# Identity shuffles in place of VectorE copies in a sliding-window kernel

## The chip, the core and the metric

One core of a Trainium2 chip. The metric is device time in microseconds (us) of one execution, the median of the runs. All runs compared here are at a granted clock of 1.00.

## The reference

All 8 x 8 windows at stride 4 of 16 x 64 images of 64 x 64 float32, copied into an output with the windows outermost:

```
n_h = (h - window_size) // stride + 1          # 15
n_w = (w - window_size) // stride + 1          # 15
for i in range(n_h):
    for j in range(n_w):
        result[:, i, j] = x[:, :, i*4 : i*4+8, j*4 : j*4+8].copy()     # 64 channels x 8 x 8
```

There is no arithmetic: 16.8 MB come in, 59 MB of windows go out.

## The kernel before

The image lies in `L`, spread over 128 partitions: 2 channel halves x 16 images x 4 bands of 16 rows. For each store tile `G` (one of four buffers, 16 KB per partition) ScalarE (`act`) and VectorE (`dve`) gather one window per partition, then GpSimd issues an indirect store that sends each partition's 16 KB to its place in the output. A unit with `s = 0` ("plain") handles windows that lie within one band in both halves. A "cross" unit (`s = 2`) pairs windows of one half within a band with windows of the other half (`s = 3`) whose last 4 rows lie in the next band, that is in the next partition; those rows are fetched by a `stream_shuffle` with the mask `nxt`. The 16 rows of a cross unit that have no window are dropped by the store's bounds check.

```
def fill(g, half, s, j, lo, n, copies):
    d = slice(half * HP + lo, half * HP + lo + n)          # 64 partitions
    cols = slice(j * ST, j * ST + WS)
    for ch in (half, 1 - half):
        ...
        copy = copies[ch != half]
        if s < NSLOT - 1:
            copy(out=g[d, cs, :, :], in_=L[f, :, s * ST : s * ST + WS, cols])       # 2048 elements
        else:
            copy(out=g[d, cs, 0:ST, :], in_=L[f, :, s * ST : RB, cols])             # 1024 elements
            nc.vector.stream_shuffle(out=g[d, cs, ST:WS, :], in_=L[f, :, 0:ST, cols], mask=nxt)

def unit(j, s):
    g = tile_()                                  # next of the 4 buffers
    if s == 0:
        for half in range(CH):
            fill(g, half, half, j, 0, HP, (act, dve))
        scatter(g, idx, j, s)
    else:
        turn = crossed % 2
        crossed += 1
        fill(g, turn, s, j, 0, HP, (act, act))
        fill(g, 1 - turn, s + 1, j, 0, HP, (dve, dve))
        scatter(g, (idx_hi, idx_lo)[turn], j, s)
# ... six early tiles, three plain units between them, then 3 cross + 1 plain, five times ...
j = NW - 1                                       # the tail: two half-filled tiles
tile_()                                          # one buffer is skipped
for s in range(2):
    g = tile_()
    # ... act and dve copy 32 x 2048 twice each; 4 stores of 256 KB from the SP and ACT queues ...
```

## Time and profile before

| | before |
|---|---|
| median of the first 3 runs (range) | 191.89 us (191.82 to 192.07) |
| VectorE busy | 120.5 us of 190.1 |
| ScalarE busy | 130.0 us |
| data moved | 75.81 MB, mean 399 GB/s |
| steady rate, 78 to 166 us | 421 GB/s |

No engine is busy even 70% of the span, while the transfer engines are busy in nearly all of it. The lines stand in the prediction.

### The profile page before, as it was taken

The page shows a single profiled execution, that of the slowest core. Times are in us where ns is not written, and L with a number is a line of the kernel's source. Part 1 is how long each engine was busy: PE and PEld are TensorE (multiplying, and loading weights), DVE is VectorE, ACT ScalarE, POOL GpSimd, SP SyncE. Part 2 cuts the span into 40 slices and gives each one's busy share as a digit, 9 for nine tenths or more (in the row PEclk, how much of TensorE's full clock was granted, in tenths as well). Part 3 has the DMA queues.
Part 4 walks back from the last instruction along what each step waited for, and adds up shares of the span by engine and source line. Part 5 has one row for each costly group of instructions (what it writes and reads, how often), then busy time and mean ns, then how long its engine had stood idle before and what let it go on. Part 6 is the DMA issues. An engine that isn't in the chain of part 4 may idle for free.

```text
span 190.1 us, 481 instructions
## 1 busy us (share of the span) xinstructions
DVE 120.5 (63%) x160; ACT 130.0 (68%) x69; POOL 49.9 (26%) x50
## 2 busy tenths in 40 slices
DVE  4000007999998969877659586795877679552420
ACT  0000007999999989977779589797877979572750
POOL 7402203205535321522322222223122431210000
DMA  2999999999999999999999999999999999999974
GB/s 83 310 408 403 398 400 396 400 401 392 438 431 431 422 424 441 417 410 417 441 397 431 426 422 414 424 438 393 438 414 417 428 424 424 405 434 410 421 331 197
DMA packets 11156, 75.81 MB, mean 399 GB/s; under 512 B 3456, under 2 KB 3456, under 8 KB 7552
## 3 DMA queue, kind: packets, MB, share of 16 engines
q0 software_dynamic: 9040, 66.34, 84.7%
q1 hardware_dynamic: 2048, 8.91, 12.0%
q10 hardware_dynamic: 64, 0.52, 0.7%
q14 instruction: 4, 0.03, 0.0%
HBM read 16.78 MB, written 62.91 MB: 419 GB/s over the span
## 4 chain that ended last, share of the span: by engine, by line
DMA 84%; DVE 6%; ACT 3%; POOL 2%; issue 1%; ACTq 0%; DVEq 0%; PEldq 0%
DMA out_dram<-G,idx_hi 30%; DMA L<-in_x_dram 20%; DMA out_dram<-G,idx 14%; DMA out_dram<-G,idx_y 13%; DMA out_dram<-G,idx_lo 7%; DVE G L166 4%; POOL L L58 2%; ACT G L212 2%; ACT G L143 1%; DVE G L146 1%; DVE G L145 0%; DVE G L143 0%; POOL pi L69 0%; ACTq L143 0%; DVEq L145 0%
## 5 line engine op out<-in xcount | busy, mean ns | idle before, releaser
L143 ACT COPY G<-L 64x2048 f32<-64x2048 f32 x46 | 87.2, 1896 | 17.0 <-DMA out_dram<-G,idx_hi 7.6
L166 DVE COPY G<-L 32x2048 f32<-32x2048 f32 x30 | 36.9, 1230 | 28.9 <-DMA L<-in_x_dram 25.9
L146 DVE STREAM_SHUFFLE G<-L 64x1024 f32<-64x1024 f32 x30 | 38.3, 1276 | 0.0
L166 ACT COPY G<-L 32x2048 f32<-32x2048 f32 x18 | 33.9, 1896 | 1.2 <-DMA out_dram<-G,idx_y 0.8
L145 DVE COPY G<-L 64x1024 f32<-64x1024 f32 x30 | 20.6, 688 | 16.4 <-DMA out_dram<-G,idx_hi 10.5
L143 DVE COPY G<-L 64x2048 f32<-64x2048 f32 x16 | 19.6, 1223 | 6.7 <-DMA out_dram<-G,idx 6.3
L166 ACT ACT_TABLE_LOAD x1 | 1.3, 1283 | 29.5 <-DMA L<-in_x_dram 29.5
L123 POOL DMA_INDIRECT out_dram<-G,idx_y x6 | 10.8, 1808 | 25.2 <-DVE G L166 24.1
L58 POOL DMA_DIRECT2D L<-in_x_dram x16 | 10.9, 695 | 24.1 <-DMA L<-in_x_dram 23.6
L123 POOL DMA_INDIRECT out_dram<-G,idx_hi x8 | 9.7, 1207 | 24.2 <-DVE G L146 12.3
L123 POOL DMA_INDIRECT out_dram<-G,idx_lo x7 | 8.0, 1144 | 29.4 <-DVE G L146 19.6
L123 POOL DMA_INDIRECT out_dram<-G,idx x8 | 10.2, 1270 | 18.0 <-ACT G L143 18.0
L212 ACT COPY G<-L 32x2048 f32<-32x2048 f32 x4 | 7.6, 1897 | 5.5 <-DMA out_dram<-G,idx_lo 4.5
L212 DVE COPY G<-L 32x2048 f32<-32x2048 f32 x4 | 4.9, 1220 | 8.2 <-DMA out_dram<-G,idx_lo 5.8
L72 DVE TENSOR_SCALAR tb<-pi 128x1 int32<-128x1 int32 x1 | 0.2, 155 | 1.0 <-POOL pi L69 1.0
L78 DVE TENSOR_TENSOR th<-tc,tq 128x1 int32<-128x1 int32 x2 | 0.3, 156 | 0.0
L75 DVE TENSOR_SCALAR th<-tc 128x1 int32<-128x1 int32 x2 | 0.3, 154 | 0.0
L69 POOL IOTA pi<- 128x1 int32 x1 | 0.1, 124 | 0.4 <-PEq L246 0.4
L146 DVE LOAD_MASK_SELECT G<-L x30 | 0.2, 6 | 0.0
L78 DVE CUSTOM_DVE_ANT_0 tb<-tb,th 128x2 uint16<-128x2 uint16 x1 | 0.2, 160 | 0.0
L78 DVE CUSTOM_DVE_ANT_0 idx_y<-idx_y,idx 128x2 uint16<-128x2 uint16 x1 | 0.2, 160 | 0.0
L78 DVE CUSTOM_DVE_ANT_0 idx<-tb,th 128x2 uint16<-128x2 uint16 x1 | 0.2, 159 | 0.0
(16 smaller groups left out, 2.2 us busy)
## 6 DMA issues: line engine op xcount, KB each, us to landing
L<-in_x_dram POOLq DMA_DIRECT2D x8, 1024.0 KB, 21.1
L<-in_x_dram SPq DMA_DIRECT2D x8, 896.0 KB
out_dram<-G SPq DMA_DIRECT2D x6, 256.0 KB
L<-in_x_dram POOLq DMA_DIRECT2D x8, 128.0 KB, 21.2
out_dram<-G ACTq DMA_DIRECT2D x2, 256.0 KB
out_dram<-G,idx POOLq DMA_INDIRECT x8, 14.7
out_dram<-G,idx_hi POOLq DMA_INDIRECT x8, 14.6
out_dram<-G,idx_lo POOLq DMA_INDIRECT x7, 12.9
```

Of the source, the lines that this page charges most:

```text
L58: eng.dma_start(out=L[p0 : p0 + QP - HQ + 1 : HQ, c0:c1, :, :], in_=x_v[ch, y, q, :, c0:c1, :])
L69: nc.gpsimd.iota(pi[:, :], pattern=[[0, 1]], base=0, channel_multiplier=1)
L72: nc.vector.tensor_scalar(out=d[:, :], in0=pi[:, :], scalar1=shift, scalar2=mask, op0=ALU.logical_shift_right, op1=ALU.bitwise_and)
L75: nc.vector.tensor_scalar(out=d[:, :], in0=a[:, :], scalar1=float(m), scalar2=None, op0=ALU.mult)
L78: nc.vector.tensor_tensor(out=d[:, :], in0=a[:, :], in1=b[:, :], op=op)
L123: st = nc.gpsimd.indirect_dma_start(out=o_v, out_offset=bass.IndirectOffsetOnAxis(ap=ix[:, 0:1], axis=0), in_=g.rearrange("p c r w -> p (c ...
L143: copy(out=g[d, cs, :, :], in_=L[f, :, s * ST : s * ST + WS, cols])
L145: copy(out=g[d, cs, 0:ST, :], in_=L[f, :, s * ST : RB, cols])
L146: nc.vector.stream_shuffle(out=g[d, cs, ST:WS, :], in_=L[f, :, 0:ST, cols], mask=nxt)
L166: (act if (2 * d + ch) % 3 == 0 else dve)(out=g[d * QP : (d + 1) * QP, ch * CL : (ch + 1) * CL, :, :], in_=L[f : f + QP, :, s * ST : s * S ...
L212: copy(out=g[d, ch * CL : (ch + 1) * CL, :, :], in_=L[f, :, s * ST : s * ST + WS, cols])
```

## The change

In the kernel before, GpSimd takes 0.96 us at its shortest to issue a store, and up to 2.37 us beside VectorE's copies. The prediction reads this, from the page of the Trainium skill named in its point (2), as a lock: a fast copy keeps GpSimd from writing the descriptors of its stores, and a slower shuffle doesn't. A shuffle with an identity mask moves the same data (1.28 us for 1024 elements, where the copy takes 0.69). The intent is to keep GpSimd's issues short in the steady part. Since VectorE's work grows, ScalarE takes a quarter of the channels of the second move.

```
+    same = list(range(32))
+    def shf(out, in_):
+        nc.vector.stream_shuffle(out=out, in_=in_, mask=same)
+    def mix(out, in_):
+        k = out.shape[1] // 4
+        act(out=out[:, 0:k], in_=in_[:, 0:k])
+        shf(out=out[:, k:], in_=in_[:, k:])
...
-    def unit(j, s):
+    def unit(j, s, fast=False):
...
-            for half in range(CH):
-                fill(g, half, half, j, 0, HP, (act, dve))
+            fill(g, 0, 0, j, 0, HP, (act, dve if fast else shf))
+            fill(g, 1, 1, j, 0, HP, (act, dve if fast else mix))
...
-            fill(g, 1 - turn, s + 1, j, 0, HP, (dve, dve))
+            fill(g, 1 - turn, s + 1, j, 0, HP, (shf, mix))
...
-        unit(*plain.pop(0))                # the three units among the early tiles
+        unit(*plain.pop(0), fast=True)
```

## The prediction

> **What bounds the kernel now.** I read the page first, then the windows (busy time by stretch), then the timeline of the steady part, and last the tile view of the output. On the page, part 2 gives the answer at once:
>
> ```profile
> ## 2 busy tenths in 40 slices
> DVE  4000007999998969877659586795877679552420
> ACT  0000007999999989977779589797877979572750
> DMA  2999999999999999999999999999999999999974
> GB/s 83 310 408 403 398 400 396 400 401 392 438 431 431 422 424 441 417 410 417 441 397 431 426 422 414 424 438 393 438 414 417 428 424 424 405 434 410 421 331 197
> ```
>
> The row to look at is DMA: 9 in every slice from the second to the 38th, while VectorE (DVE) and ScalarE (ACT) fall to 5 to 8 once the loads are over (slice 17 on). Some 76 MB have to move, and the transfer engines never pause for want of work except in the last two slices. The chain that ended last says the same:
>
> ```profile
> DMA 84%; DVE 6%; ACT 3%; POOL 2%; issue 1%; ACTq 0%; DVEq 0%; PEldq 0%
> ```
>
> The windows ask whether the transfer rate depends on what VectorE does. The columns are the stretch, its length, busy time of DVE, ACT and POOL (GpSimd), clock, DMA share, GB/s:
>
> ```profile
> 170.00:175.00 5.00, 0.30 (x1) 0.55 (x2) 0.96 (x1) 1.00 1.00 419
> 46.00:78.00 32.00, 28.50 (x24) 30.61 (x17) 13.03 (x8) 1.00 1.02 428
> 78.00:166.00 88.00, 66.25 (x98) 71.69 (x38) 23.30 (x20) 1.00 1.01 421
> ```
>
> It doesn't. With VectorE 89% busy, nearly all of it plain copies, the rate is 428 GB/s; with copies and shuffles mixed 421; with VectorE almost idle 419. The share is 1.00 each time. So the steady part (about 78 to 175 us) is bound by the rate of the transfers, and a fill matters only if it comes too late to keep one store waiting behind another. How late may it come?
>
> ```profile
> DMA to landing us min/median/max: 8.2/13.8/15.1
> ```
>
> In the tile view the first store, issued at 44.5 us with nothing of its own kind ahead, landed after 8.2 us; a steady one takes 13.8. The difference, 5.6 us, is time that a store spends behind the ones ahead of it: slack in the queue.
>
> **What the Trainium skill says.** (1) "VectorE: DVE Perf Modes", section on the perf-mode tier table: a float32 copy of 2048 elements between SBUF tiles runs in a doubled mode, 1227 ns; STREAM_SHUFFLE has only a single-rate form, about 2400 ns. The trace agrees where it can: copies of 2048 take 1223 ns, the existing shuffles of 1024 take 1276. (2) "SBUF — State Buffer", section on who interferes with whom: a two-port copy on VectorE locks GpSimd out of a shared port pair, so descriptors of a transfer issued from GpSimd wait; single-rate instructions don't. The trace fits: a store's issue takes 957 ns at its shortest, and 1.73 to 2.37 us in the worst cases, which lie beside copies. This lock is clearly what the change is after. (3) "HBM Reference", Specifications: a core streaming alone gets about 425 GB/s, bounded by its 16 DMA engines. The steady part is at 421, so hardly 1% is left there. (4) "VectorE: DVE Perf Modes", section on the TRN2 errata: a ScalarE SBUF copy costs 224 cycles plus one per element at 1.2 GHz. For 2048 that is 1893 ns; the trace has 1896.
>
> **The change part by part.** It touches 20 of the 31 store tiles: 5 "plain" units (s = 0) and all 15 "cross" units. The costs of today are in part 5 of the page:
>
> ```profile
> L143 ACT COPY G<-L 64x2048 f32<-64x2048 f32 x46 | 87.2, 1896 | 17.0 <-DMA out_dram<-G,idx_hi 7.6
> ...
> L146 DVE STREAM_SHUFFLE G<-L 64x1024 f32<-64x1024 f32 x30 | 38.3, 1276 | 0.0
> ...
> L145 DVE COPY G<-L 64x1024 f32<-64x1024 f32 x30 | 20.6, 688 | 16.4 <-DMA out_dram<-G,idx_hi 10.5
> L143 DVE COPY G<-L 64x2048 f32<-64x2048 f32 x16 | 19.6, 1223 | 6.7 <-DMA out_dram<-G,idx 6.3
> ```
>
> One cross unit in the timeline, from its buffer coming free to its store being issued:
>
> ```profile
> 87.31 0.69 DVE L145 COPY G<-L 64x1024 f32<-64x1024 f32 x1 [1.00 <-DMA out_dram<-G,idx_y]
> 87.31 3.82 ACT L143 COPY G<-L 64x2048 f32<-64x2048 f32 x2 [1.06 <-DMA out_dram<-G,idx_y]
> 87.93 0.01 DVE L146 LOAD_MASK_SELECT G<-L  x1
> 87.93 1.28 DVE L146 STREAM_SHUFFLE G<-L 64x1024 f32<-64x1024 f32 x1
> 89.24 0.69 DVE L145 COPY G<-L 64x1024 f32<-64x1024 f32 x1
> 89.86 0.00 DVE L146 LOAD_MASK_SELECT G<-L  x1
> 89.86 1.28 DVE L146 STREAM_SHUFFLE G<-L 64x1024 f32<-64x1024 f32 x1
> 91.91 1.73 POOL L123 DMA_INDIRECT out_dram<-G,idx_hi  x1 [3.78 <-DVE G L146]
> ```
>
> Both engines start together; VectorE ends at 91.14 (3.83 us), ScalarE at 91.13, and the store follows 0.77 us later.
>
> Shuffle costs: 1024 elements, 1.28 us (trace). From that and the skill's 2.40 us at 2048, a straight line gives 0.15 us plus 1.10 us per 1024: about 1.00 us at 768 and 1.84 us at 1536 (estimates from the page "VectorE: DVE Perf Modes" and the trace). ScalarE's quarter by the errata formula: 0.40 us for 256, 0.61 us for 512 elements (estimates).
>
> - Cross unit, VectorE: removed 2 copies, added shuffles of 1024 and 768. Now 1.28 + 1.28 + 1.00 + 1.28 = 4.84 us, with some 0.03 us between instructions 4.94. Before 3.83: +1.1. ScalarE: 3.82 + 0.40 = 4.2 us.
> - Plain unit, VectorE: 2.40 + 1.84 + gaps = 4.3 us, before 2.47. ScalarE: 3.82 + 0.61 = 4.43, before 3.82: +0.6 for the fill.
> - Removed on GpSimd: the lock. An issue should fall to 0.96 us each time. In the steady part that is worth 0.2 us on average, at most 0.8, of a latency of 13.8 that has 5.6 of slack: nothing at the end.
>
> The sum that decides: VectorE's new work in the 20 units is 15 x 4.94 + 5 x 4.3 = 95.6 us (before 15 x 3.85 + 5 x 2.5 = 70). It can start at 77.6 us, when the first cross unit's buffer comes free, and it's next needed at 174.7 us, when the store of the 18th of these units has landed and frees the first tail tile's buffer. That is 97.1 us. So VectorE goes from about three quarters busy to 98%, and still just fits. The last plain unit would be issued near 174.7 us where it was 170.5; with the 8.2 us of an empty queue it could land by 182.9, before the 185.1 at which it lands now (170.5 + 14.6). The queue loses some 4 of its 5.6 us of slack and the transfers keep going. Transfers still set the end: **no gain, no loss, or a loss of a few tenths**.
>
> **The rivals.**
> A. *The lock costs transfers now, and the change frees them (faster).* For: issues that take 2 us beside copies. Against: 428 GB/s in just the stretch that is full of copies, DMA share 1.00. If the steady rate went from 421 to the skill's 425, the 97 us would shrink by 0.9 us: about 191.
> B. *VectorE becomes the bound (slower).* The margin is 1.5 us of 97, and the shuffle durations at 768, 1536 and 2048 aren't in the trace. If each shuffle costs 5% more than I think, VectorE is 3 to 5 us late at the tail, part of which the queue hides: 193 to 195. Also for it: the 16 transfer engines aren't evenly loaded (a cross store leaves out 16 rows of one half; at 180 to 185 us, with a store still unfinished, the window shows a DMA share of only 0.74), so a shorter queue may let the early ones run dry. I charge 0.3 us for this.
> C. *A new wait between engines (slower).* In a cross unit ScalarE writes rows 0 to 3 of 8 channels among whose rows 4 to 7 VectorE's last shuffle writes. If the dependency tracking takes these interleaved writes for an overlap, that shuffle waits for ScalarE's quarter (end 4.2 us into the unit, shuffle due at 3.6): 0.6 us x 15 = 9 us on an engine with no room, about 197. I think the tracking is exact: one in ten.
> D. *The tail moves.* The tail tiles' copies aren't changed; they wait for buffers (5.8 us on VectorE). Unless B happens they start at the same time.
>
> **How the numbers follow.** 191.9 plus 0.3 for the shorter queue: 192.2 us. Low end 190.4, a bit below A. High end 195.0, the far end of B. Two per cent faster would be 188.1 us, 3.8 us that no stretch of the profile has to give: 0.04. Two per cent slower, 195.7, needs C or the bad end of B: 0.09. Within 2%: 0.87.
>
> **What would show it.** In the changed profile: (1) the DMA row still 9 throughout and 420 GB/s in the steady part; falling shares mean B. (2) Shuffle groups of 2.4, 1.84, 1.28 and 1.0 us and ScalarE quarters of 0.61 and 0.40. (3) Store issues by GpSimd from 78 us on all near 0.96 us; if not, the lock wasn't their cause. (4) Median landing shorter, 10 to 13 us, falling along the run, with the end unmoved. (5) VectorE at 9 in nearly all slices 17 to 36, and no wait of VectorE for ScalarE in the list of waits (else C). I'm wrong if the steady rate itself rises well above 425 GB/s, for then the copies were costing the transfers something that these windows don't show, or if the last fills come later than about 177 us.

## The result, and the profile after

The changed kernel takes 191.69 us (191.46 to 192.06, 6 runs); the kernel before, run beside it, 191.94 (191.54 to 192.29, 6 runs). The ratio is 0.9989, with a 95% interval of 0.9973 to 1.0005: the same. Here and below a ratio is the mean time of one kernel's fast runs over that of the other's fast runs of the same rounds, so it isn't quite the ratio of the medians quoted.

The profile has changed much more than the time. Part 2 of the changed kernel's page, busy tenths in 40 slices:

```profile
DVE  4000007999998969899989999999999999995420
ACT  0000007999999979988889889999898699993750
DMA  2999999999999999999999999999999999999984
```

VectorE is now at 9 in nearly every slice to the 36th, and the DMA row is the same but for one tenth in slice 39. The windows of the steady part and of the stretch in which VectorE used to be idle (columns as in the prediction):

```profile
78.00:166.00 88.00, 85.55 (x133) 80.33 (x57) 18.28 (x19) 1.00 1.01 422
170.00:175.00 5.00, 2.62 (x3) 1.46 (x3) 0.96 (x1) 1.00 1.00 419
```

VectorE is busy 97% of the steady part where it was busy 75% (66.25 of 88), and the rate is 422 GB/s where it was 421. The groups of the steady part by form, as count, busy time, mean ns of one:

```profile
L146 DVE STREAM_SHUFFLE G<-L 64x1024 f32<-64x1024 f32 x30 | 38.4, 1282 | 0.0
...
L153 DVE STREAM_SHUFFLE G<-L 64x1024 f32<-64x1024 f32 x15 | 19.2, 1279 | 0.5
L153 DVE STREAM_SHUFFLE G<-L 64x768 f32<-64x768 f32 x15 | 15.0, 998 | 0.5
L153 DVE STREAM_SHUFFLE G<-L 64x2048 f32<-64x2048 f32 x5 | 12.2, 2434 | 0.1
...
L153 DVE STREAM_SHUFFLE G<-L 64x1536 f32<-64x1536 f32 x5 | 9.3, 1863 | 0.2
...
L157 ACT COPY G<-L 64x256 f32<-64x256 f32 x15 | 6.0, 403 | 0.4
...
L157 ACT COPY G<-L 64x512 f32<-64x512 f32 x5 | 3.1, 616 | 0.1
```

L153 is the identity shuffle, L157 ScalarE's quarter. One cross unit in the timeline (mask loads and the lines of the units beside it left out):

```profile
101.76 3.82 ACT L143 COPY G<-L 64x2048 f32<-64x2048 f32 x2
...
102.28 1.28 DVE L153 STREAM_SHUFFLE G<-L 64x1024 f32<-64x1024 f32 x1
...
103.48 1.27 DVE L146 STREAM_SHUFFLE G<-L 64x1024 f32<-64x1024 f32 x1
...
104.78 1.00 DVE L153 STREAM_SHUFFLE G<-L 64x768 f32<-64x768 f32 x1
105.60 0.40 ACT L157 COPY G<-L 64x256 f32<-64x256 f32 x1
...
105.69 1.27 DVE L146 STREAM_SHUFFLE G<-L 64x1024 f32<-64x1024 f32 x1
...
107.73 0.96 POOL L123 DMA_INDIRECT out_dram<-G,idx_hi  x1 [3.39 <-DVE G L146]
```

There are three things to see. GpSimd's issue takes 0.96 us, the shortest in either trace: the lock is gone. VectorE's first instruction has no idle note in brackets, nor has the mask load ahead of it: the buffer was already free, so VectorE runs from one unit straight into the next. And the last shuffle starts at 105.69 while ScalarE's quarter runs until 106.00, so VectorE doesn't wait for ScalarE where the two engines' writes interleave.

The chain that ended last looks quite different:

```profile
DMA 54%; DVE 33%; issue 6%; POOL 2%; ACT 2%; DVEq 0%; PEldq 0%; ACTq 0%
```

Transfers had 84% of it and VectorE 6%. Read alone, this says that VectorE became a third of the bound, yet the time is the same. A chain shows which of two paths came last at each step, not by how much. By how much is told by the time from issue to landing of the stores issued from 140 to 166 us, first of the kernel before and then of the changed one:

```profile
DMA to landing us min/median/max: 12.9/14.4/15.1
```

```profile
DMA to landing us min/median/max: 10.5/11.6/12.4
```

Stores wait 2.8 us less behind others. The fills come later, and the queue is shorter by just that; the transfers don't notice.

### The profile page after: what moved, and what is told of

The parts are those of the page before. It is cut to its first block, busy times and chain, and to the rows that moved or that the text cites. A ratio compares the mean times of both kernels' runs of the same rounds, so it can differ in the third digit from the quotient of the medians.

```text
span 190.0 us, 556 instructions
## 1 busy us (share of the span) xinstructions
DVE 142.7 (75%) x200; ACT 139.2 (73%) x89; POOL 45.7 (24%) x50
## 3 DMA queue, kind: packets, MB, share of 16 engines
q1 hardware_dynamic: 2048, 8.91, 12.0%
## 4 chain that ended last, share of the span: by engine, by line
DMA 54%; DVE 33%; issue 6%; POOL 2%; ACT 2%; DVEq 0%; PEldq 0%; ACTq 0%
DMA L<-in_x_dram 21%; DVE G L153 17%; DMA out_dram<-G,idx_hi 13%; DMA out_dram<-G,idx_y 13%; DVE G L146 11%; DMA out_dram<-G,idx 7%; DVE G L176 4%; POOL L L58 2%; ACT G L222 2%; DVE G L143 0%; POOL pi L69 0%; DVEq L153 0%; DVEq L176 0%; PEldq L256 0%; ACTq L222 0%
## 5 line engine op out<-in xcount | busy, mean ns | idle before, releaser
L153 DVE STREAM_SHUFFLE G<-L 64x1024 f32<-64x1024 f32 (+3 forms) x40 | 55.6, 1391 | 1.3
L123 POOL DMA_INDIRECT out_dram<-G,idx_hi x8 | 7.7, 962 | 30.6 <-DVE G L146 19.2
L123 POOL DMA_INDIRECT out_dram<-G,idx x8 | 9.1, 1136 | 19.9 <-ACT G L157 10.6
L123 POOL DMA_INDIRECT out_dram<-G,idx_lo x7 | 6.7, 962 | 27.4 <-DVE G L146 19.0
L157 ACT COPY G<-L 64x256 f32<-64x256 f32 (+1 forms) x20 | 9.1, 456 | 0.5
L143 DVE COPY G<-L 64x2048 f32<-64x2048 f32 x6 | 7.3, 1222 | 0.2
L153 DVE LOAD_MASK_SELECT G<-L x40 | 0.5, 12 | 2.1 <-DMA out_dram<-G,idx_y 0.9
```

The lines of the kernel that those rows point to most:

```text
L123: st = nc.gpsimd.indirect_dma_start(out=o_v, out_offset=bass.IndirectOffsetOnAxis(ap=ix[:, 0:1], axis=0), in_=g.rearrange("p c r w -> p (c ...
L153: nc.vector.stream_shuffle(out=out, in_=in_, mask=same)
L157: act(out=out[:, 0:k], in_=in_[:, 0:k])
```

## The experiments

The theory is that the transfers set the end, and that both the lock and the longer fills lie in the slack of the store queue. The main rival is that two real effects cancel: the lock did cost time, its removal gained it, and VectorE's longer work gave it back. The experiments below undo one at a time, overload VectorE in two doses, and take the slack away.

**1. Neither lock nor long fill (wrong result).** Only 2 of 32 channels are moved by VectorE's two row moves; ScalarE's quarter is dropped.

```
-        nc.vector.stream_shuffle(out=out, in_=in_, mask=same)
+        nc.vector.stream_shuffle(out=out[:, 0:2], in_=in_[:, 0:2], mask=same)
 ...   # and mix() is shf() alone
```

> The changed kernel with VectorE's two row moves per unit cut to 2 of 32 channels and ScalarE's quarter dropped (wrong result on purpose: the rest of the tile holds old rows, the stores are the same size). So in the steady part there is neither the lock of a two-port copy nor a long fill on VectorE. Theory (transfers set the end, fills lie in the queue's slack): 191.7 us, within 0.3% of both kernels, landing back near 13.8 to 15 us. Rival (the copies' lock cost transfers, and the change gave the gain back through VectorE's longer work): 190.5 us or less, steady rate over 425 GB/s.

Measured: 191.67 us (191.59 to 191.70, 5 runs), 0.9983 of the kernel before (0.9970 to 0.9996). VectorE's busy time falls from 142.7 to 97.2 us, every steady issue takes 0.96 us, and the median landing from 140 to 166 us is 14.0 us. The window of the steady part:

```profile
78.00:166.00 88.00, 45.40 (x137) 72.19 (x39) 19.01 (x20) 1.00 1.00 420
```

With both costs removed 0.2% is gained, 0.3% at most by the interval. The rival asked for 190.5 us or less and over 425 GB/s; it falls.

**2. Same VectorE time, with the lock.** Each identity shuffle becomes the same copy done twice.

```
-        nc.vector.stream_shuffle(out=out, in_=in_, mask=same)
+        for _ in range(2):
+            nc.vector.tensor_copy(out=out, in_=in_)
```

> The changed kernel with each identity shuffle replaced by the same copy done twice: VectorE's time per unit stays nearly the same (2 x 0.62 to 0.69 us in place of 1.2 to 1.3 us)[...]. Theory: 191.7 us, within 0.3% of the changed kernel; GpSimd's issues lengthen to 1.2 to 2.4 us but lie in the slack. Rival (the lock matters): 193 us or more.

Measured: 191.39 us (190.92 to 191.49, 6 runs), 0.9965 of the kernel before (0.9952 to 0.9978). VectorE is busy 143.0 us against 142.7 of the changed kernel. The window of the steady part:

```profile
78.00:166.00 88.00, 85.76 (x135) 80.29 (x58) 21.35 (x19) 1.00 1.01 422
```

Busy times and rate are those of the changed kernel; only GpSimd's time is up (21.35 us against 18.28), because some issues stretch again beside copies, up to 1.77 us. The lock is there and costs nothing. This kernel is even 0.2% ahead of the changed one; its interval and that kernel's overlap only just (0.9973 to 0.9978), and what makes the difference is not settled.

**3 and 4. More work on VectorE, in two doses.** Without ScalarE's quarter:

```
     def mix(out, in_):
-        k = out.shape[1] // 4
-        act(out=out[:, 0:k], in_=in_[:, 0:k])
-        shf(out=out[:, k:], in_=in_[:, k:])
+        shf(out=out, in_=in_)
```

> The changed kernel without ScalarE's quarter: VectorE gets 0.28 us more in each of 15 cross units and 0.57 us more in each of 5 plain ones, 7.0 us in all. Theory: VectorE would end its last steady unit near 179 us where the tail's first buffer comes free at about 174.5, so the slack is used up and part of the 7 us shows: 192.5 to 195 us, landing down to about 8 to 9 us at the end. Rival (there is more slack than 5.6 us, or VectorE's time is not on any path): 191.7 us.

With the second shuffle of each unit done twice:

```
         shf(out=out[:, k:], in_=in_[:, k:])
+        shf(out=out[:, k:], in_=in_[:, k:])
```

> The changed kernel with the second shuffle of each unit done twice (same result): 0.91 us more in each of 15 cross units and 1.75 us more in each of 5 plain ones, 22.4 us in all, so that VectorE must be the bound. Theory: VectorE ends its last steady unit near 194 us, then the last store lands 8 us and more later: 202 to 206 us; the first 3 to 6 us of the 22.4 are hidden by the slack, landing near 8 us from the middle on, DMA share below 0.95. Rival (not slack but something else hid the change's work): it stays hidden here too, or all 22.4 us show (214 us).

Measured:

| | VectorE busy over the changed kernel's 142.7 us | median time | over the changed kernel's 191.69 us | hidden |
|---|---|---|---|---|
| without the quarter | 149.7, +7.0 us | 193.92 us (193.75 to 194.13) | +2.2 us | 4.8 us |
| second shuffle twice | 165.4, +22.7 us | 209.69 us (209.31 to 209.93) | +18.0 us | 4.7 us |

(The kernel before took 191.90 us in these rounds and 191.94 in those of the changed kernel, so the differences may be taken.) Both doses hide the same amount. Beyond it the time grows one for one: from the first to the second, 15.7 us more work cost 15.8 us. That amount is the slack that the changed kernel has left. The median landing without the quarter, stores issued from 140 to 166 us:

```profile
DMA to landing us min/median/max: 7.1/7.5/8.4
```

With the second shuffle twice the median is 7.0 us from 100 us on, and the transfers starve:

```profile
78.00:166.00 88.00, 86.88 (x139) 71.76 (x52) 15.06 (x16) 1.00 0.86 364
```

Issues are 5.6 us apart here, so at most the last 1.3 us of one store lie ahead of the next. About 7.0 us is thus what a store takes with nearly nothing ahead of it, and the changed kernel's 11.6 us holds 4.6 us of waiting: the same number as the 4.7 to 4.8 us found by overloading. The first dose came out within its range. For the second I had said 202 to 206 us; it was 209.7. VectorE was done with the last steady unit at 193.0 us and that unit's store had landed by 202.5, as I had said. What I left out are the two tail tiles: VectorE copies its share of them only after that, until 198.0 us, and their stores land by 206.6.

**5 and 6. No slack: two store buffers in place of four.**

```
-    NG = 4
+    NG = 2
```

> The kernel before with 2 store buffers in place of 4, so that a store has at most one other ahead of it and there is no slack: each unit takes half of fill + 0.77 us + about 7 us to landing. Theory: (3.85 + 0.77 + 7.0) / 2 = 5.8 us per cross unit, far above the 4.5 us of the transfers; with the early tiles about 235 us (225 to 245), DMA share below 0.85 in the steady part. Rival (transfers set the end whatever the buffers): below 200 us.

> The changed kernel with 2 store buffers in place of 4. Theory: the longer fill (4.75 against 3.85 us in a cross unit, 4.45 against 3.85 in a plain one) is now on the path and costs half of itself, or all where the two buffers' fills follow one another: (0.9 x 15 + 0.6 x 5) / 2 = 8 us over the kernel before with 2 buffers, at most 16. Rival (the lock costs transfers and the shuffles free them): faster than the kernel before with 2 buffers.

Measured: 239.38 us (239.22 to 239.59) for the kernel before, 245.67 us (245.38 to 245.74) for the changed one: 6.3 us, or 2.6%, slower. The windows from 110 to 220 us, first before and then changed:

```profile
110.00:220.00 110.00, 64.21 (x92) 70.65 (x38) 20.45 (x18) 1.00 0.76 318
```

```profile
110.00:220.00 110.00, 79.61 (x123) 73.80 (x53) 16.64 (x18) 1.00 0.72 305
```

With at most one other store outstanding the transfers are busy only three quarters of the time, landing takes 7.0 to 7.1 us at the median, and the longer fill costs time: a cross unit's takes 4.7 us in place of 3.8. That is the cost that four buffers hide. The 6.3 us are below the 8 that I had worked out as half of the longer fills. The lock's removal could account for some of that, since issues are shorter here too; these two runs don't part the two.

**7 and 8. Earlier stores in the tail.** The profile before has a DMA share of only 0.74 at 180 to 185 us, which looks like time to be won. Without the skipped buffer the two tail tiles are filled earlier.

```
     j = NW - 1
-    tile_()
```

> The kernel before without the skipped tile ahead of the tail: the two tail tiles take the buffers of the 17th and 18th steady unit, which come free near 170 and 175 us, in place of those of the 18th and 19th. Theory: the end is set by the transfers, so what can still be won is where they have too little to do (DMA share 0.74 at 180 to 185 us, 1.3 us of transfer time): 190.5 us (189.7 to 191.2). Rival (the tail's dip is engines of unequal load, which no earlier store can fill): 191.9 us.

> The changed kernel without the skipped tile ahead of the tail. Theory: as for the kernel before without it, but VectorE and ScalarE are done with the last steady unit only at 171.9 us, so the tail tiles are filled by 174.5 and 178.5 us: 190.5 us (189.7 to 191.2), the same as the kernel before without the skip within 0.3%. Rival (unequal load): 191.7 us.

Measured: 192.96 us, 1.0052 of the kernel before (1.0040 to 1.0064), and 192.47 us, 1.0030 (1.0017 to 1.0043). Both are slower, by 0.5 and 0.3%, so my reading of the tail was wrong. The rival's numbers (191.9 and 191.7 us, no gain) were missed too. The last windows of the kernel before without the skip:

```profile
180.00:185.00 5.00, 0.00 (x0) 0.00 (x0) 0.00 (x0) 1.00 0.99 419
185.00:188.00 3.00, 0.00 (x0) 0.00 (x0) 0.00 (x0) 1.00 0.52 219
```

The dip didn't vanish but moved: the share is now full until 185 us, where it was 0.74, and half after it, where it was 0.91. The last indirect store, issued at about the same time, lands after 17.8 us in place of 14.6. The packed trace keeps 16 landing signals for every store. For the last indirect store of the kernel before, eight come by 180.5 us and the other eight from 183.4 to 185.1 us. Without the skip, eight come by 181.5 us and the others from 186.4 to 188.5. The share of 0.52 in the last row fits: half of the 16 transfer engines have more left than the other half. That is the unequal load of my rival; why half of them lag isn't shown.

The same traces show why the end comes later. GpSimd's closing instruction, a drain, ends 1.9 us after the last indirect store has landed, in all 13 kept traces. In the kernel before that is at 187.0 us, ahead of the last tail store's landing at 189.15. Without the skip it is at 190.4 us, behind the tail stores' 189.3, and the span grows from 190.1 to 191.2 us. In the changed kernel without the skip it comes last too (189.8 us against 188.8). So the earlier tail stores delay the last indirect store, and the program then ends with that one.

**9 to 11. An even share in the tail.** ScalarE gives 6 of its 32 channels of a tail tile to VectorE, so that a tile is filled in 3.18 us in place of 3.82.

```
-            for ch, copy in enumerate((act, dve)):
+            for ch, c0, c1, copy in ((0, 0, 26, act), (0, 26, CL, dve), (1, 0, CL, dve)):
```

> The kernel before with the copies of the two tail tiles shared evenly: ScalarE gives 6 of its 32 channels to VectorE, so that a tail tile is filled in about 3.2 us in place of 3.82. Theory (the only transfer time left to win is in the tail, where the DMA share is 0.74 at 180 to 185 us): the last stores are issued 0.6 us earlier; 191.4 us (191.0 to 191.7), 0.1 to 0.5% faster. Rival (the dip is unequal load of the transfer engines): 191.9 us.

> The changed kernel with the same even tail. Theory: 191.2 us (190.8 to 191.5), the same step as for the kernel before. Rival: 191.7 us.

> The kernel with each identity shuffle replaced by the same copy done twice (191.39 us when first run), with the same even tail. If its 0.2% ahead of the changed kernel was real and the tail's gain adds to it: 190.9 us (190.5 to 191.2). If it was chance: as the changed kernel with the even tail.

Measured: 191.96 us, 0.9995 of the kernel before (0.9982 to 1.0009); 191.46 us, 0.9971 (0.9957 to 0.9985); and 191.41 us, 0.9964 (0.9950 to 0.9977). On the kernel before the even tail does nothing: the last store's issue is over at 185.3 us in place of 185.8, but it lands at 189.11 in place of 189.15. I had said 191.4 us; the rival's 191.9 came out. With copies done twice it adds nothing to run 2 (I had said 190.9 us), and is level with the changed kernel with the even tail, which I had named beforehand as the sign that run 2's lead was chance. The changed kernel with the even tail is ahead of the kernel before by 0.3%, with an interval clear of 1 and within the range that I gave. Against the changed kernel (0.9973 to 1.0005) the intervals overlap, so it isn't shown to beat both. No version tried is more than 0.4% from the kernel before, unless it overloads VectorE, has too few buffers, or has the tail's buffers changed.

## Why the prediction was right

- **The bound.** Transfers set the end before and after: 421 and 422 GB/s in the steady part, DMA share 1.01 in both.
- **The costs.** Shuffles of 2048, 1536, 1024 and 768 elements were put at 2.40, 1.84, 1.28 and 1.00 us and take 2.43, 1.86, 1.28 and 1.00. ScalarE's quarters were put at 0.61 and 0.40 us and take 0.62 and 0.40.
- **VectorE's sum.** 95.6 us were predicted from 77.6 us on. The trace has the first of these shuffles at 77.99 us and the last ending at 171.91: 93.9 us, waits included. A cross unit takes 4.7 us and not 4.94: I had added 0.03 us between instructions, but a shuffle's successor starts up to 0.1 us before the shuffle's reported end (103.48 against 102.28 + 1.28). So the last plain store was issued at 172.7 us and not at 174.7.
- **The slack.** This was the mis-sized term. I took the 8.2 us of the first store as an empty queue's, though the input was still being loaded beside it (until about 47 us in the trace). That gave 5.6 us, and expected some 4 us of it to be used. The experiments put an empty queue's landing at 7.0 us, so the slack late in the steady part was 7.4 us (14.4 - 7.0). The change used 2.8 of it and left 4.6. Both errors leaned to the cautious side; the margin was wider than I thought.
- **The lock.** Issues fell to 0.96 us each, and that was worth nothing, as said; run 2 puts the lock back at no loss.
- **The rivals.** A falls by runs 1 and 2. B didn't happen, but it is close: run 3 reaches it with 7.0 us more on VectorE. C didn't happen: the shuffle at 105.69 us doesn't wait for ScalarE's quarter. D held: the first tail tile starts at 174.20 us, before at 174.68.
- **The 0.3 us for the shorter queue** didn't show: the median moved by -0.25 us, within the spread of the runs. The dip at 180 to 185 us that I gave as a reason for it exists, and so does the unequal load of the transfer engines; runs 7 and 8 show that filling the dip gains nothing.
- **Two slips that changed nothing.** The straight line through 1.28 and 2.40 us is 0.16 us plus 1.12 per 1024 elements, not 0.15 plus 1.10; the four costs taken from it are right. And VectorE's row doesn't stay at 5 to 8 from slice 17 on: some slices are at 9.

## What to carry to other kernels

Where transfers set the pace, as here, ask of a lock, a wait or a slower engine whether the queue behind it runs dry; the time from issue to landing, less what it is with an empty queue, says how much can be hidden. Measure that slack by adding a known amount of work to the suspect and seeing how much of it doesn't show: two doses that hide the same amount are good evidence. And when the chain of waits changes its make-up but not its length, two paths may be nearly equal (here they were within some 5 us), and neither share is a measure of what could be gained.

## What the Trainium skill lacked or had wrong

- "SBUF — State Buffer", the box on VectorE blocking DMA: it says that the DMA engines sit idle while GpSimd is locked out. Here issues did stretch to 1.7 and 2.4 us beside copies, but with other stores already queued the transfer engines' mean share stayed at 1.01 to 1.02: 428 GB/s with VectorE 89% busy, mostly copies, and 422 GB/s with every steady identity shuffle replaced by a copy done twice. The page lacks that stores already issued hide the lock.
- "VectorE: DVE Perf Modes", the perf-mode tier table: it gives one size for STREAM_SHUFFLE, about 2400 ns at 2048 elements. The runs agree (2434 ns) and add 1863 ns at 1536, 1279 at 1024, 998 at 768 and, from run 1, 221 at 64.
- No page that I read says how late a fill may come when stores queue. Here a 1.84 to 2.10 MB indirect store lands about 7.0 us after its issue with nearly nothing ahead of it, and four buffers gave 7.4 us on top of that as slack.
